# RWKV-7 recurrence with its output by time steps on partitions, group norm along the free axis, and later weight splits

## The chip, the cores and the metric

The kernel runs on one core of one Trainium2 chip. The metric is the device time in microseconds of one execution; the time shown is the median of several runs. The engines have queues of their own, which run in order: TensorE (PE), VectorE (DVE), ScalarE (ACT), GpSimd (POOL), and SyncE (SP), which issues most of the DMAs.

## The reference, cut to what matters

Two decoder layers over 512 prompt tokens and 8 samples of one token each (520 columns, N). Each layer is a norm, one input projection of 53 tiles of 128 output channels, sliding-window attention in 16 heads beside an RWKV-7 recurrence in 16 heads, SiLU gates, and one output projection of 16 tiles. The change touches the recurrence's output and the group norm behind it:

```python
def step(S, inp):
    r_t, w_t, k_t, v_t, kk_t, a_t = inp
    sa = jnp.einsum('bhij,bhj->bhi', S, -kk_t)
    S = (S * w_t[:, :, None, :] + sa[..., None] * (kk_t * a_t)[:, :, None, :]
         + v_t[..., None] * k_t[:, :, None, :])
    return S, jnp.einsum('bhij,bhj->bhi', S, r_t)
...
mu = jnp.mean(ys, axis=-1, keepdims=True)
var = jnp.mean(jnp.square(ys - mu), axis=-1, keepdims=True)
yn = ((ys - mu) * lax.rsqrt(var + GN_EPS)).reshape(Bn, T, RWKV_WIDTH)
yn = yn * ln_w.astype(f32) + ln_b.astype(f32)
bonus = jnp.sum(r_h * k_h * r_k.astype(f32), axis=-1, keepdims=True) * v_h
y_rw = (yn + bonus.reshape(Bn, T, RWKV_WIDTH)).astype(x.dtype)
```

`ys` has 64 channels for each head; the mean and the variance go over them. The result is then multiplied by a gate.

## The kernel before, in words

**The projections.** Activations lie with channels on partitions and the 520 columns along the free axis. Weights come as fp32 blocks of 4 x 128 rows by 128 columns ("quarters", four for each output tile). Each is split into a rounded part `hi` and a rest `lo`; activations are split likewise (`hh`, `hl`; in the output projection `yh`, `yl`). `quarter` (L372 to L387) does 4 x 3 x 2 matmuls of 260 columns in fp32r into an accumulator. After the last one it calls `split_w(n + DEPTH)`: ScalarE casts the `hi` of the quarter after that (L355), VectorE subtracts to give `lo` (L365), SP loads a later one (L347). `lo` has three buffers, `hi` four and the raw blocks four. `held` names quarters of the second layer's first two tiles, which are used in two passes over half the columns, 12 matmuls each.

**The side work.** All else is written as generators (`chain`, `attend`, `attend_samples`, `gate`, `ada` and others) that `Side` threads between the projection's matmuls. After each such matmul but an accumulator's last, `tick` advances a count and runs at most one generator to its next `yield`; the number that it yields is its distance in ticks to its next piece. `W` holds these distances. `drain` runs pieces without matmuls between until a condition holds. So the order of instructions in each engine's queue is written out when the kernel is built, and only data and buffers make engines wait.

**The order of tiles** in a layer: the low-rank tile L, then for each pair of heads p three tiles P (r, k, v), with gate tiles R and A among them, then K, V, K, V, eight Q, and the rest of the gate tiles A. After the tile A3 the kernel goes on through A4 to A7, and drains the last attention and the chains behind A4, and the sample attention behind A7. Then comes the output projection; its first half of input channels are those of the recurrence.

**A chain** (`chain`, from L535) is started for each pair of heads after its third P tile, 16 chains in all; about three are under way at a time. It makes decays and keys, 64 x 64 products (`atp`, L638), the masked `atq` and `atk`, writes `atk` to DRAM and loads it again as `f` on GpSimd's DMA queue (L662), inverts 32 x 32 triangles on GpSimd (L670, L672, in `xi`), sends the inverse back through DRAM into `xT` (L714, L721), and completes it with two groups of small matmuls (`t2a`, L733 and L741) with copies on VectorE between them (L727, L736, L745).

Then it goes through eight blocks of 64 time steps (L747 to L789). In each, `rp` (L763) is the product of the stacked (q, kk) of the block with the state `m0`; only its lower half is read. `sp` (L770) applies the inverse. `mn` (L774) is the update of the state. The output `yp` is made with channels on partitions: L775 has all 128 columns of `sv` as stationary side and `atq` (128 columns) as moving side, and L777 adds the state's part with `m0` stationary. ScalarE copies two 64 x 64 blocks into `y` (L787).

Behind the blocks come the eight samples' states, whose outputs are put into the last 8 columns of `y` (L819, L823). The group norm goes over all 520 columns with channels on partitions: `y` is split, centred by a product with `cmat` (`yc`, four matmuls of 260 columns), squared, split, summed by `bones` (`vp`, four more), and the root is taken on ScalarE as `Ln` and `Exp` (L842, L843). VectorE scales and adds weight, bias and bonus (L845, L847) and multiplies with the gate (L851).

**Buffers.** Most tiles of up to 520 columns come from one ring `t2` of `NW2` buffers; matmul outputs of the side work from four PSUM banks (`ps1`).

Of the kernel before, what the change touches and what calls it, by code (L numbers as in the profile page):

```python
# [27 lines left out]
NW2 = 71  # L28
# [78 lines left out]
DEPTH = 3  # L107
RMS = 29
HQ = 4
LEAD0 = 3  # L110
GA = 1
# [60 lines left out]
def body(ctx, tc, xt, ct, consts, pars, wada, win, wout, lora, sst, swkv, ck, cv, cvn, fing,  # L172
# [62 lines left out]
    bia = cpool.tile([128, 1], F32, name="bia")  # L235
    ve.memset(bia, 64 * GN_EPS)
# [7 lines left out]
    lnw8 = cpool.tile([128, L, 8], F32, name="lnw8")  # L244
    nsk = cpool.tile([128, L, 17], F32, name="nsk")

    def derive(mats):
# [7 lines left out]
        ve.tensor_scalar(out=lnw8, in0=par[:, :, P_LNW:P_LNW + 8], scalar1=8.0, scalar2=None, op0=ALU.mult)  # L255
# [86 lines left out]

    def load_w(n):
# [155 lines left out]
    def layer(l, hh, hl, xprev, xnext, start, prepare, after):  # L499
# [35 lines left out]
        def chain(p, lw, r, kr, v):  # L535
# [55 lines left out]
            ve.scalar_tensor_tensor(out=rk, in0=r, scalar=pc(P_RK), in1=k, op0=ALU.mult, op1=ALU.mult)  # L591
# [36 lines left out]
            atq, atk = [], []  # L628
# [96 lines left out]
            x1 = sm.tile([128, 2, 8, 32], F32, tag="x1", name="x1", bufs=1)  # L725
# [11 lines left out]
            yield W[30]  # L737
# [8 lines left out]
            yield W[31]  # L746
            y = t2([128, N], "y")  # L747
            for c in range(8):
# [11 lines left out]
                yp = ps[:, 384:512].rearrange("p (h t) -> p h t", h=2)  # L760
# [35 lines left out]
            yield W[35]  # L796
# [17 lines left out]
            sy.dma_start(out=o_ss[l, p], in_=st)  # L814
            yield W[38]
            ps = ps1("ys")

            for b in range(0, B, 2):
                pe.matmul(ps[:, 2 * b:2 * b + 4], st[:, b:b + 2].rearrange("p b i -> p (b i)"),  # L819
                          rbd[:, b:b + 2].rearrange("p b h -> p (b h)"), start=True, stop=True)  # L820
            for h in range(2):
                for i in range(2):
                    ve.tensor_copy(y[64 * h:64 * h + 64, T + i:N:2], ps[64 * i:64 * i + 64, 2 * i + h:2 * B:4])  # L823
            yield W[39]

            yh = high(y)
            yield W[40]
            ys = low(y, yh)
            yield W[41]
            ycs = t2([128, N], "ycs")  # L830
            s2 = y
            for h in range(2):
                se.copy(out=ycs[:, h * NH:(h + 1) * NH], in_=sums(cmat, ys, h, "yc"))
                yield W[42]
            se.activation(out=s2, in_=ycs, func=AF.Square)
            s2h = high(s2)
            yield W[43]
            s2s = low(s2, s2h)
            yield W[44]
            vps = [sums(bones, s2s, h, "vp") for h in range(2)]  # L840
            for h in range(2):
# [652 lines left out]
```

## Time and profile before

| | before |
|---|---|
| median of 3 runs | 2344.32 us (2335.37 to 2345.83) |
| profiled execution, its own time | 2349.78 us |
| its span, first to last instruction | 2348.0 us |
| mean granted TensorE clock, of full speed | 0.975 |
| TensorE busy | 2223.8 us, 20708 matmul instructions |
| VectorE busy | 1482.8 us |
| ScalarE busy | 1057.9 us |
| GpSimd busy | 794.7 us |

The rows further down are from that one profiled execution; all their times count from its first instruction. Matmuls are pipelined, so the duration of one is longer than its distance to the next; the distance of starts is what it costs in a stream. An fp32 matmul is two instructions, a transpose and an fp32r matmul one.

### The profile page before, as it was taken

The numbers are of one execution on the slowest core, as the hardware profiler recorded it, in microseconds if no ns is written. First come the engines' busy times: TensorE is split into PE (matmuls) and PEld (weight loads), VectorE is DVE, ScalarE is ACT, GpSimd is POOL, SyncE is SP. The second block draws the span as 40 slices with busy tenths as digits, with TensorE's granted clock in tenths as the row PEclk, the third lists the DMA queues.
The fourth block names the chain that finished last, engine by engine and source line by source line (L and its number), as shares of the span: only waits on it lengthen the run. The fifth ranks groups of instructions, "written<-read, shape, count | busy, mean of one in ns | idle before, by whom it ended". The sixth has DMA issues, their size and how long they took to land. (4 is left out here: it accounts for less than half of the span.)

```text
span 2348.0 us, 53897 instructions
## 1 busy us (share of the span) xinstructions
PE 2223.8 (95%) x20708; PEld 2104.7 (90%) x20708; DVE 1482.8 (63%) x3712; ACT 1057.9 (45%) x2346; POOL 794.7 (34%) x1428
## 2 busy tenths in 40 slices
PE   5999999999999999999999999999999999999997
PEld 4899989999989898889989989889999999899997
DVE  3464677767785886533365456577776778765346
ACT  3244354554455555422244435345555446553222
POOL 2105655766566000000011526655776440000112
PEclk8999999999999999999999999999999999999998
DMA  9945555323333225777762455543332322244335
GB/s 363 348 149 169 166 158 160 104 89 97 102 95 95 64 79 158 225 225 245 244 211 77 129 156 163 165 138 106 94 96 88 96 90 77 60 131 138 113 115 180
DMA packets 229329, 337.92 MB, mean 144 GB/s; under 512 B 59696, under 2 KB 80304, under 8 KB 228912
## 3 DMA queue, kind: packets, MB, share of 16 engines
q1 hardware_dynamic: 223184, 321.89, 44.1%
q0 software_dynamic: 5888, 12.59, 1.8%
q8 instruction: 163, 2.67, 0.5%
q14 instruction: 94, 0.77, 0.1%
HBM read 303.90 MB, written 32.56 MB: 143 GB/s over the span
## 5 line engine op out<-in xcount | busy, mean ns | idle before, releaser
L365 DVE TENSOR_TENSOR lo<-raw,hi 128x512 fp32r<-128x512 f32 x568 | 414.5, 730 | 454.0 <-PE psO L380 135.4
L355 ACT CAST hi<-raw 128x512 fp32r<-128x512 f32 x568 | 350.8, 619 | 632.2 <-PE psP L380 211.2
L380 PE MATMUL psP<-hh,lo 128*128 128x260 f32 x1408 | 307.7, 292 | 0.0
L380 PE MATMUL psP<-hl,hi 128*128 128x260 f32 x1408 | 305.0, 292 | 0.0
L380 PE MATMUL psP<-hh,hi 128*128 128x260 f32 x1408 | 304.1, 292 | 0.2 <-ACT dm L518 0.2
L672 POOL TENSOR_TENSOR xi<-xi,tmp 128x248 f32<-128x248 f32 (+30 forms) x496 | 280.8, 566 | 38.9
L670 POOL TENSOR_TENSOR tmp<-f,xi 128x248 f32<-128x248 f32 (+30 forms) x496 | 258.7, 521 | 86.6 <-DMA f<-d 49.1
L380 PEld LDWEIGHTS psP<-hh,lo 128*128 128x128 f32 x1408 | 225.7, 192 | 6.3 <-issue 3.7
L380 PEld LDWEIGHTS psP<-hl,hi 128*128 128x128 f32 x1408 | 225.1, 192 | 5.9 <-issue 3.3
L380 PE MATMUL psO<-yh,hi 128*128 128x260 f32 x1024 | 225.1, 286 | 3.6 <-DVE xsn L1193 3.6
L380 PEld LDWEIGHTS psP<-hh,hi 128*128 128x128 f32 x1408 | 224.6, 192 | 3.1 <-issue 1.2
L380 PE MATMUL psO<-yh,lo 128*128 128x260 f32 x1024 | 225.2, 286 | 1.7 <-DVE lo L365 1.7
L380 PE MATMUL psO<-yl,hi 128*128 128x260 f32 x1024 | 224.5, 285 | 0.0
L380 PEld LDWEIGHTS psO<-yh,hi 128*128 128x128 f32 x1024 | 166.6, 191 | 5.7 <-issue 5.6
L380 PEld LDWEIGHTS psO<-yh,lo 128*128 128x128 f32 x1024 | 166.7, 191 | 3.6 <-DVE lo L365 1.9
L380 PEld LDWEIGHTS psO<-yl,hi 128*128 128x128 f32 x1024 | 166.6, 191 | 1.6 <-issue 1.6
L1329 POOL TENSOR_SCALAR yo<-xnew,fg 128x260 f32<-128x260 f32 x32 | 31.2, 978 | 391.6 <-DVE xnew L1190 377.4
L445 POOL TENSOR_TENSOR rmsr<-rmsv,mhalf 128x3 f32<-128x3 f32 x6 | 5.6, 938 | 464.4 <-DMA raw<-in_wout_dram 449.3
L787 ACT COPY y<-seq 64x64 f32<-64x64 f32 x256 | 52.6, 205 | 195.5 <-DVE mbd L781 136.1
L299 PE MATMUL adps<-rawa,cT 128*32 128x128 f32 (+1 forms) x2048 | 112.5, 348 | 23.5 <-DMA rawa<-in_wada_dram 23.0
L380 PE MATMUL psQ<-hl,hi 128*128 128x260 f32 x512 | 117.6, 295 | 0.0
L380 PE MATMUL psQ<-hh,lo 128*128 128x260 f32 x512 | 114.3, 294 | 0.0
(362 smaller groups left out, 5463.6 us busy)
## 6 DMA issues: line engine op xcount, KB each, us to landing
raw<-in_win_dram SPq DMA_DIRECT2D x424, 256.0 KB, 3.3
rawa<-in_wada_dram SPq DMA_DIRECT2D x384, 256.0 KB, 4.8
raw<-in_wout_dram SPq DMA_DIRECT2D x152, 256.0 KB, 3.6
f<-d POOLq DMA_DIRECT2D x64, 128.0 KB, 3.6
gd<-th SPq DMA_DIRECT2D x22, 260.0 KB, 2.5
gr<-gd SPq DMA_DIRECT2D x22, 260.0 KB, 3.5
x<-in_xt_dram SPq DMA_DIRECT2D x16, 260.0 KB, 5.3
yd<-rk SPq DMA_DIRECT2D x16, 260.0 KB, 3.4
```

The costliest lines, as they stand in the source:

```text
L299: pe.matmul(ap[32 * g:32 * g + 32, 0:w], cT[:, kk, :], raw[g * w // 512][:, c:c + w], start=(kk == 0), stop=(kk == KT - 1))
L355: se.copy(out=his[n], in_=raws[n])
L365: ve.tensor_tensor(out=lo, in0=raws.pop(n), in1=hi, op=ALU.subtract)
L380: pe.matmul(ps[:, h, 0:NH], a[:, k % 4], b[:, h * NH:(h + 1) * NH], start=(k == k0 and j == 0), stop=stop)
L445: ge.tensor_tensor(out=r[:, 0:3], in0=v[:, 0:3], in1=mhalf[:, 0:3], op=ALU.pow)
L670: ge.tensor_tensor(out=tv, in0=f[:, s:s + 1, s + 1:32].to_broadcast([128, 8, 31 - s]), in1=xi[:, :, s:s + 1].to_broadcast([128, 8, 31 - s] ...
L672: ge.tensor_tensor(out=xi[:, :, s + 1:32], in0=xi[:, :, s + 1:32], in1=tv, op=ALU.add)
L787: se.copy(out=y[hs, 64 * c:64 * c + 64], in_=yp[hs, h])
L1329: ge.tensor_scalar(out=out[h][m // 2][:, m % 2], in0=xn[:, h * NH:h * NH + NH], scalar1=fg[:, m:m + 1], scalar2=None, op0=ALU.mult)
```

## The change

- **Output of a block by time steps.** `ap` has 64 time steps on partitions and 2 x 64 channels along the free axis: for each head a slice of `aqs` of 72 columns (64 of `atq` and 8 beyond) is the stationary side, 64 columns of `sv` the moving one. `aqs` is `atq` with 8 more columns, the last 8 set to zero. L777 goes; the state's part is the upper half of `rp`, which ScalarE copies into `yq`. `y` and `yq` hold block c on partitions 64 (c % 2) and on, at column group c // 2. GpSimd adds them after the eighth block.
- **Group norm along the free axis.** For the 512 prompt columns, mean and variance come from `bn_stats` and `bn_aggr` on VectorE, eight of each, the root from a power on GpSimd, and scale and shift are done by eight `Identity` activations on ScalarE; four transposes bring `y` back to channels on partitions, and one instruction on VectorE scales it and adds it to the bonus `b2`. The 8 samples keep the old way in 8 columns (`ysm`), with the power in place of `Ln` and `Exp`. The factors 0.5, ln_w and ln_b are folded into constants (`hrk`, `hln`, `lnw4`).
- **Weight splits.** `quarter` puts the split on a list `due`; the next quarter carries it out behind its ninth matmul (`LATE`).
- **Distances and buffers.** 40 ticks more ahead of the load of `f`; `W[30]` doubled, `W[31]` times four (the `t2a` groups); `W[35]` + 10, and 8 and 4, around the statistics; the last distances of the chain shorter; `W[79]` tripled for the second `qq` subtraction in `attend`; `W[61]` tripled in `attend_samples`; `GA` 2 in place of 1 (tiles of `ada` loaded ahead for the gate's modulation); `NW2` 72 in place of 71; `x1` moves into the ring.

```diff
-NW2 = 71
+NW2 = 72
...
+LATE = 9
...
-GA = 1
+GA = 2
...
@@ quarter
+        done = 0
         for k in range(4 * key[1], 4 * key[1] + 4):
...
+                    done += 1
+                    if done == LATE and due:
+                        split_w(due.pop())
...
         if key not in held or not halves[0]:
-            split_w(n + DEPTH)
+            due.append(n + DEPTH)
@@ chain
             for g in range(2):
-                atq.append(t2([128, 4, 2, 64], "atq"))
+                aq = t2([128, 520], "atq")
+                ge.memset(aq[:, 512:520], 0.0)
+                aqs.append(aq)
+                atq.append(aq[:, 0:512].rearrange("p (e h t) -> p e h t", e=4, h=2))
...
+            yield 40
             for j in range(4):
                 ge.dma_start(out=f[j:128:4], in_=d1.rearrange("b c s t -> (b c) s t"))
...
-            yield W[30]
+            yield 2 * W[30]
...
-            yield W[31]
-            y = t2([128, N], "y")
+            yield 4 * W[31]
+            y = t2([128, 4, 128], "y")
+            yq = t2([128, 4, 128], "yq")
+            ge.memset(yq[0:64, 0], 0.0)
...
                 if c:
                     pe.matmul(rp, qk[g][:, e].rearrange("p a t -> p (a t)"), m0, start=True, stop=True)
                     ve.tensor_tensor(out=rr[64:128], in0=rp[64:128], in1=sv[g][64:128, e], op=ALU.add)
+                    se.copy(out=yq[ys, c // 2], in_=rp[0:64])
...
-                pe.matmul(yp, sv[g][:, e], atq[g][:, e], start=True, stop=(c == 0))
-                if c:
-                    pe.matmul(yp, m0, qk[g][:, e, 0].unsqueeze(1).to_broadcast([128, 2, 64]), start=False, stop=True)
+                for h in range(2):
+                    o = 128 * e + 64 * h
+                    w = 72
+                    pe.matmul(ap[0:w, 64 * h:64 * h + 64], aqs[g][:, o:o + w], sv[g][:, e, 64 * h:64 * h + 64],
+                              start=True, stop=True)
...
-                for h in range(2):
-                    hs = slice(64 * h, 64 * h + 64)
-                    se.copy(out=y[hs, 64 * c:64 * c + 64], in_=yp[hs, h])
+                se.copy(out=y[ys, c // 2], in_=ap[0:64])
                 yield W[34]
+            ge.tensor_tensor(out=y, in0=y, in1=yq, op=ALU.add)
...
-            yield W[35]
+            yield W[35] + 10
+            for i in range(8):
+                ve.bn_stats(out=st6[:, i], in_=y[:, i // 2, 64 * (i % 2):64 * (i % 2) + 64])
+            yield 8
+            for i in range(8):
+                ve.bn_aggr(out=mv[:, i], in_=st6[:, i])
+            ve.tensor_scalar(out=mv[:, :, 0], in0=mv[:, :, 0], scalar1=-1.0, scalar2=None, op0=ALU.mult)
+            ve.tensor_scalar(out=rs8, in0=mv[:, :, 1], scalar1=GN_EPS, scalar2=None, op0=ALU.add)
+            ge.tensor_tensor(out=rs8, in0=rs8, in1=mhalf, op=ALU.pow)
+            yield 4
+            ge.tensor_tensor(out=mv[:, :, 0], in0=mv[:, :, 0], in1=rs8, op=ALU.mult)
...
+            for i in range(8):
+                yi = y[:, i // 2, 64 * (i % 2):64 * (i % 2) + 64]
+                se.activation(out=yi, in_=yi, func=AF.Identity, scale=rs8[:, i:i + 1], bias=mv[:, i, 0:1])
             yield W[38]
...
+            ps = ps1("yT")
+            for j in range(4):
+                pe.transpose(ps[:, 128 * j:128 * j + 128], y[:, j], ident)
+            ve.scalar_tensor_tensor(out=b2[:, 0:T], in0=ps, scalar=hln[:, l, p:p + 1], in1=b2[:, 0:T], op0=ALU.mult,
+                                    op1=ALU.add)
             yield W[39]
-            yh = high(y)
...
-            ys = low(y, yh)
...
-                se.copy(out=ycs[:, h * NH:(h + 1) * NH], in_=sums(cmat, ys, h, "yc"))
...
-            se.activation(out=s2, in_=ycs, func=AF.Square)
-            s2h = high(s2)
...
-            vps = [sums(bones, s2s, h, "vp") for h in range(2)]
...
-                se.activation(out=s2[:, h * NH:(h + 1) * NH], in_=vps[h], func=AF.Ln, bias=bia[:, 0:1])
-            se.activation(out=s2, in_=s2, func=AF.Exp, scale=-0.5)
...
+            ps = ps1("yc")
+            pe.matmul(ps[:, 0:B], cmat.bitcast(F32), ysm[:, 0], start=True, stop=True)
...
+            pe.matmul(ps[:, 0:B], bones.bitcast(F32), ysm[:, 2], start=True, stop=True)
...
@@ attend
-                yield W[79]
+                yield W[79] * (1 + 2 * u)
@@ attend_samples
-                yield W[61]
+                yield 3 * W[61]
```

## Rows read from the trace of the kernel before

**Rows 1.** The page, part 1: busy time, share of the span, instructions.

```profile
PE 2223.8 (95%) x20708; PEld 2104.7 (90%) x20708; DVE 1482.8 (63%) x3712; ACT 1057.9 (45%) x2346; POOL 794.7 (34%) x1428
```

**Rows 2.** TensorE's waits: for whom, us in total, times, longest.

```profile
PE adps L299 <- DMA rawa<-in_wada_dram: 23.0, 9, 17.7
PE t2a L741 <- DVE x L736: 14.6, 9, 2.2
PE seq L774 <- DVE sv L772: 12.9, 12, 2.0
...
PE sc L949 <- DVE qq L931: 5.6, 7, 2.0
...
PE psS L380 <- DVE part L404: 3.6, 2, 1.8
PE psO L380 <- DVE xsn L1193: 3.6, 2, 1.8
...
PE ssc L1041 <- DMA ktc<-in_ck_dram: 1.8, 1, 1.8
```

**Rows 3.** Two windows: busy by engine, TensorE's granted clock, DMA share, GB/s.

```profile
1625.00:1635.00 10.00, 10.00 (x115) 9.47 (x114) 9.51 (x21) 2.89 (x6) 1.04 (x1) 1.00 0.37 101
1637.60:1641.00 3.40, 3.40 (x31) 3.36 (x24) 1.22 (x4) 0.24 (x1) 1.85 (x4) 0.67 0.62 207
```

**Rows 4.** TensorE's timeline, a block of the recurrence: start, duration, line, shapes, count.

```profile
1616.29 0.38 PE L774 MATMUL seq<-sv,kbt 128*128 128x128 f32 x2
1616.51 0.39 PE L775 MATMUL seq<-atq,sv 128*128 128x128 f32 x2
...
1617.07 0.40 PE L380 MATMUL psP<-hh,hi 128*128 128x260 f32 x2
1617.31 0.40 PE L380 MATMUL psP<-hl,hi 128*128 128x260 f32 x2
```

**Rows 5.** TensorE's timeline, the samples' output (one projection matmul left out).

```profile
329.36 0.95 PE L819 MATMUL ys<-rbd,st 128*128 128x4 f32 x8
...
330.38 0.40 PE L380 MATMUL psP<-hh,hi 128*128 128x260 f32 x2
```

**Rows 6.** TensorE's timeline, the samples' attention (one projection matmul left out).

```profile
2121.09 0.40 PE L1067 MATMUL spo<-sptb,vc 128*64 128x4 f32 x8
...
2121.65 0.40 PE L380 MATMUL psA<-hh,lo 128*128 128x260 f32 x2
```

**Rows 7.** TensorE's timeline, four transposes (two projection matmuls left out).

```profile
889.55 0.60 PE L982 MATMUL pT<-cst,s 128*128 128x128 f32 x4
...
890.23 0.40 PE L380 MATMUL psQ<-hl,hi 128*128 128x260 f32 x2
```

**Rows 8.** ScalarE's timeline, a chain's group norm.

```profile
883.88 1.28 ACT L842 ACT_TABLE_LOAD   x1
...
887.88 0.84 ACT L985 COPY ptb<-pT 128x512 f32<-128x512 f32 x2
```

**Rows 9.** TensorE's timeline at the same place.

```profile
888.50 0.67 PE L993 MATMUL ops<-ptb,vtok 128*64 128x128 f32 x8 [2.12 <-ACT ptb L985]
```

**Rows 10.** VectorE's timeline, second layer's output projection.

```profile
2164.60 0.69 DVE L365 TENSOR_TENSOR lo<-raw,hi 128x512 fp32r<-128x512 f32 x1 [2.20 <-PE psO L380]
2165.21 0.87 DVE L1190 SCALAR_TENSOR_TENSOR xnew<-psO,mod,xo 128x260 f32<-128x260 f32 x2
...
2166.19 0.17 DVE L1194 TENSOR_TENSOR xsn<-xsn,xo 128x8 f32<-128x8 f32 x1
```

**Rows 11.** The chain that ended last, end of the input projection: start, us, what.

```profile
2136.56 0.41 PE pnb L1075 x2
2136.96 4.47 PE psA L380 x37
```

**Rows 12.** GpSimd's timeline between two chains' inversions.

```profile
1556.69 1.04 POOL L659 TENSOR_TENSOR kb<-kb,pend 128x512 f32<-128x512 f32 x1 [4.33 <-issue]
...
1566.45 2.16 POOL L662 DMA_DIRECT2D f<-d  x4 [8.71 <-DMA d<-atk]
```

More of the change, by code (lines that the diff above doesn't have):

```diff
@@ L234, in body @@
     bones, cmat, rotm = sel[:, 0], sel[:, 1], sel[:, 2]
-    bia = cpool.tile([128, 1], F32, name="bia")
-    ve.memset(bia, 64 * GN_EPS)
     mhalf = cpool.tile([128, 8], F32, name="mhalf")
@@ L243, in body @@
     oka = cpool.tile([128, L, 8], F32, name="oka")
-    lnw8 = cpool.tile([128, L, 8], F32, name="lnw8")
+    hrk = cpool.tile([128, L, 8], F32, name="hrk")
+    hln = cpool.tile([128, L, 16], F32, name="hln")
+    lnw4 = cpool.tile([128, L, 8], F32, name="lnw4")
     nsk = cpool.tile([128, L, 17], F32, name="nsk")
@@ L254, in derive @@
         ve.tensor_scalar(out=oka, in0=hka, scalar1=-1.0, scalar2=1.0, op0=ALU.mult, op1=ALU.add)
-        ve.tensor_scalar(out=lnw8, in0=par[:, :, P_LNW:P_LNW + 8], scalar1=8.0, scalar2=None, op0=ALU.mult)
+        ve.tensor_scalar(out=hrk, in0=par[:, :, P_RK:P_RK + 8], scalar1=0.5, scalar2=None, op0=ALU.mult)
+        ve.tensor_scalar(out=hln, in0=par[:, :, P_LNW:P_LNW + 16], scalar1=0.5, scalar2=None, op0=ALU.mult)
+        ve.tensor_scalar(out=lnw4, in0=par[:, :, P_LNW:P_LNW + 8], scalar1=4.0, scalar2=None, op0=ALU.mult)
         ve.tensor_scalar(out=nsk, in0=par[:, :, P_SINK:P_SINK + 17], scalar1=-1.0, scalar2=None, op0=ALU.mult)
@@ L341, in body @@
     raws, his, splits = {}, {}, {}
+    due = []
     def load_w(n):
@@ L590, in chain @@
             rk = t2([128, N], "rk")
-            ve.scalar_tensor_tensor(out=rk, in0=r, scalar=pc(P_RK), in1=k, op0=ALU.mult, op1=ALU.mult)
+            ve.scalar_tensor_tensor(out=rk, in0=r, scalar=hrk[:, l, p:p + 1], in1=k, op0=ALU.mult, op1=ALU.mult)
             yield W[14]
@@ L627, in chain @@
             rks = low(rk, rkh)
-            atq, atk = [], []
+            atq, atk, aqs = [], [], []
             flat = lambda ap: ap.rearrange("p e h t -> p (e h) t")
@@ L723, in chain @@
             yield W[28]
-            x1 = sm.tile([128, 2, 8, 32], F32, tag="x1", name="x1", bufs=1)
+            x1 = t2([128, 2, 8, 32], "x1")
             for i in range(2):
@@ L745, in chain @@
                 ve.tensor_copy(flat(xT[i])[64:96, :, 32:64], pa[o:o + 32, 8:16])
-            yield W[31]
-            y = t2([128, N], "y")
+            yield 4 * W[31]
+            y = t2([128, 4, 128], "y")
+            yq = t2([128, 4, 128], "yq")
+            ge.memset(yq[0:64, 0], 0.0)
+            st6 = sm.tile([128, 8, 6], F32, tag="st6", name="st6", bufs=2)
+            mv = sm.tile([128, 8, 2], F32, tag="mv", name="mv", bufs=2)
+            rs8 = sm.tile([128, 8], F32, tag="rs8", name="rs8", bufs=2)
             for c in range(8):
@@ L759, in chain @@
                 rp, sp, mn = ps[:, 0:128], ps[:, 128:256], ps[:, 256:384]
-                yp = ps[:, 384:512].rearrange("p (h t) -> p h t", h=2)
+                ap = ps[:, 384:512]
+                ys = slice(64 * (c % 2), 64 * (c % 2) + 64)
                 rr = rrs[p % 2]
@@ L820, in chain @@
                           rbd[:, b:b + 2].rearrange("p b h -> p (b h)"), start=True, stop=True)
+            ysm = sm.tile([128, 4, B], F32, tag="ysm", name="ysm", bufs=2)
             for h in range(2):
                 for i in range(2):
-                    ve.tensor_copy(y[64 * h:64 * h + 64, T + i:N:2], ps[64 * i:64 * i + 64, 2 * i + h:2 * B:4])
+                    ve.tensor_copy(ysm[64 * h:64 * h + 64, 0, i:B:2], ps[64 * i:64 * i + 64, 2 * i + h:2 * B:4])
+            ps = ps1("yT")
+            for j in range(4):
+                pe.transpose(ps[:, 128 * j:128 * j + 128], y[:, j], ident)
@@ L824, in chain @@
+            ve.scalar_tensor_tensor(out=b2[:, 0:T], in0=ps, scalar=hln[:, l, p:p + 1], in1=b2[:, 0:T], op0=ALU.mult,
+                                    op1=ALU.add)
             yield W[39]
-            yh = high(y)
+            ps = ps1("yc")
+            pe.matmul(ps[:, 0:B], cmat.bitcast(F32), ysm[:, 0], start=True, stop=True)
+            ve.tensor_copy(ysm[:, 1], ps[:, 0:B])
+            ve.tensor_tensor(out=ysm[:, 2], in0=ysm[:, 1], in1=ysm[:, 1], op=ALU.mult)
             yield W[40]
-            ys = low(y, yh)
@@ L843, in chain @@
-            se.activation(out=s2, in_=s2, func=AF.Exp, scale=-0.5)
-            yield W[45]
-            ve.scalar_tensor_tensor(out=s2, in0=ycs, scalar=lnw8[:, l, p:p + 1], in1=s2, op0=ALU.mult, op1=ALU.mult)
-            yield W[46]
-            ve.scalar_tensor_tensor(out=b2, in0=s2, scalar=pc(P_LNB), in1=b2, op0=ALU.add, op1=ALU.add)
+            ps = ps1("vp")
+            pe.matmul(ps[:, 0:B], bones.bitcast(F32), ysm[:, 2], start=True, stop=True)
+            ve.tensor_scalar(out=ysm[:, 3], in0=ps[:, 0:B], scalar1=64 * GN_EPS, scalar2=None, op0=ALU.add)
@@ L848, in chain @@
+            ge.tensor_tensor(out=ysm[:, 3], in0=ysm[:, 3], in1=mhalf, op=ALU.pow)
+            yield 2 * W[45]
             gr = t2([128, N], "gr")
             sy.dma_start(out=gr, in_=gd[l, :, 8 + p])
-            yield W[47]
-            ve.scalar_tensor_tensor(out=b2, in0=b2, scalar=0.5, in1=gr, op0=ALU.mult, op1=ALU.mult)
+            yield W[45]
+            ve.scalar_tensor_tensor(out=ysm[:, 1], in0=ysm[:, 1], scalar=lnw4[:, l, p:p + 1], in1=ysm[:, 3],
+                                    op0=ALU.mult, op1=ALU.mult)
@@ L852, in chain @@
+            ve.tensor_tensor(out=b2[:, T:N], in0=b2[:, T:N], in1=ysm[:, 1], op=ALU.add)
+            ve.scalar_tensor_tensor(out=b2, in0=b2, scalar=hln[:, l, 8 + p:9 + p], in1=gr, op0=ALU.add, op1=ALU.mult)
             sy.dma_start(out=yd[l, :, p], in_=b2)
```

9 lines of the change are left out of this document (removed).

## The prediction

> **What bounds the kernel now.** I read the page first: TensorE is busy 2223.8 us of a span of 2348.0, VectorE 63%, ScalarE 45%, GpSimd 34% [rows 1]. That leaves TensorE 124.2 us of idle time and makes its queue the bound: time goes away only if its instructions get cheaper, or if it stands still less. Its list of waits [rows 2] says for what it stands: the largest items are single waits of 1 to 2 us behind VectorE, in the side work that is threaded between the projection's matmuls. The windows [rows 3] show a second price of such a stand: in the stretch without one the granted clock is 1.00, in the 3.4 us behind the wait of 1.48 us before the pair of `t2a` matmuls at 1637.08 it is 0.67 in the mean, part of it at the lower of the two levels (1.2 GHz of 2.4). (1.00 - 0.67) x 3.4 = 1.1 us are lost on top. [...]
>
> **1. The recurrence's matmuls.** Durations of matmuls overlap, so I take prices from starts. From 1616.29 to 1617.07 stand three fp32 matmuls of 128 stationary columns by 128 moving ones (L774, L775, L777), two instructions each, and one fp32r matmul of 260 columns, which takes 0.12 (two from 1617.07 to 1617.31) [rows 4]. (0.78 - 0.12) / 3 = 0.22 us each, 0.11 an instruction. A chain (one pair of heads in one layer; 16 in all) now pays L775 eight times and L777 seven times: 15 x 0.22 = 3.30 us. L777 goes, since the product of q with the state is already in the unused upper half of L763's output. In place of L775 come two matmuls of 72 stationary by 64 moving columns in each of 8 steps, 32 instructions. No row has that form. What sets 0.11? In `ys`, 128 stationary columns and only 4 moving ones, eight instructions and one projection matmul take 1.02 us, so (1.02 - 0.12) / 8 = 0.11 too [rows 5]: the stationary side sets it, and fewer moving columns alone would save nothing. In `spo`, 64 stationary columns, eight take (0.56 - 0.12) / 8 = 0.055 [rows 6]. Between these ends I take 0.065, nearest to `spo`, as 72 is near 64: 32 x 0.065 = 2.08 us a chain, -1.22, or **-19.5 us** for 16. With 0.055 it is -24.6; with 0.11, 3.52 a chain, it is +3.5.
>
> The Trainium skill (TensorE: Matmul & The Clock Gate, "LDWEIGHTS (loading the stationary operand)") says that a weight load's time is its columns divided by 1.2 ns, which gives an estimate of 60 ns for 72 columns and -22 us for this part; rows 5 and 6 go the same way.
>
> **2. The group norm on TensorE.** Eight fp32r matmuls of 260 columns leave each chain, 0.96 us. Four transposes come, 0.11 each: (0.68 - 0.24) / 4 [rows 7]; and two fp32 products of 128 stationary by 8 moving columns, four instructions at 0.11 [rows 5]. 0.96 - 0.88 = 0.08 a chain, **-1.3 us**.
>
> **3. The group norm on ScalarE.** Each chain now loads two tables, for `Ln` and `Exp`, 1.28 us each. With the activations they hold ScalarE from 883.88 to 887.88, 4 us, and the attention's `ptb` copy is queued behind them [rows 8]; TensorE waits 2.12 us for it at 888.50 [rows 9]. The same wait stands at 2041.12, and smaller ones of 1.46 and 0.66 elsewhere. The new norm needs no table of its own: eight short `Identity` and 15 copies in place of 16 copies and the eight wide activations and casts. **-7 us**; none of it if the eight `Identity`, waiting for GpSimd's power, block the same queue.
>
> **4. Larger distances.** The second `t2a` group comes 14 ticks (a tick is one projection matmul, 0.12 us) behind VectorE's copy instead of 7: 0.84 us off each of nine waits of 14.6 us together [rows 2], 7.6 us, and with it some of the slow stretches behind them [rows 3]: **-10 us** (0 to -18). The second `qq` subtraction gets 12 ticks more, 1.4 us, against waits of 5.6 us in seven: **-5**. The samples' `ssc` gets 8 ticks against a wait of 1.8 and one of 1.5: **-3**. Two tiles loaded ahead for the gate's modulation: of its 23.0 us, 17.7 are one wait at the start and stay, some 3 us lie in layer 1: **-3**.
>
> **5. Weight splits nine matmuls later.** VectorE and ScalarE are in-order, and now the split of a quarter's weights stands ahead of the read-out of the tile just finished. At 2164.60 `lo` (0.69 us) runs before the residual `xnew`, and TensorE waits for that accumulator [rows 10]; with the late split the read-out goes first. Four such waits, 3.6 + 3.6 us [rows 2], lose 0.7 each, 2.8, and some of their slow stretch: **-5**. The recurrence's own waits (12.9 us in twelve) keep their size in my sum, because VectorE also gets more to do: eight statistics of 64 columns, eight aggregations and nine small instructions, between 0.17 and 0.69 each [rows 10], about 4 us plus one wide add, for four wide ones of some 0.7. That is +2 us a chain, 32 us on an engine idle for 865 us [rows 1]; where the cover is missing, it becomes a recurrence wait. The late `lo` still has 44 matmuls, 5.3 us, before its quarter needs it; the weight DMA behind it on SP's queue starts 1.1 us later and has three quarters of 2.9 us.
>
> **6. What the distances cost.** The sample attention must end before the last gate tile does. Now its last product, `pnb`, has 37 projection matmuls behind it [rows 11]. Eight samples take 8 ticks more each, 64; about 12 are given back where the kernel drains the last attention. So `pnb`, `spo` and the last `spT` fall some 15 ticks past the tile's end, where no matmul covers their hand-overs to ScalarE and VectorE, which have the last gate's `tanh` and products to do: some 2.5 us of waits and one slow stretch [rows 3], 3.5 in each layer, and half a us in the drain: **+8 us**. Nothing past it is late: the first half of the output projection reads other channels.
>
> The longer chain (some 50 ticks more of about 1190) is covered: the last one starts 15 tiles of 95 ticks before its results are drained.
>
> **Sum.** -19.5 - 1.3 - 7 - 10 - 5 - 3 - 3 - 5 + 8 = -45.8. The profiled execution's own time is 2349.8, so 2304.0. That execution is 5.5 above the median of the runs; I take 2 off: **2302 us**.
>
> **The rivals.**
> *The waits come back.* VectorE's extra short instructions put new 1 to 2 us waits where the old ones were, so parts 4 and 5 give nothing: -19.5 - 1.3 - 7 + 8 = -19.8, 2330. For it: nearly all waits in rows 2 are for VectorE, in bursts. Against: the statistics are spread over 22 ticks, and the waits of part 4 get distance of their own.
>
> The Trainium skill (VectorE: DVE Perf Modes, "The TRN2 errata") speaks against the new norm: an instruction from SBUF pays a fixed cost whatever its width, so it advises tiles of 512 elements or more. The trace agrees: 0.17 us for 8 columns, 0.69 for 512 [rows 10]. By that rule eight pieces of 64 columns lose what the transposed form saves, which is this rival.
>
> *72 columns cost what 128 do.* Part 1 is +3.5: 2304 + 23 = 2327. For it: no row has such a form. Against: `spo` [rows 6].
> *Both:* 2330 + 23 = 2353: within 0.5%.
> *GpSimd becomes the pace (slower).* Its queue gets the sum `y + yq` (as `kb`, 1.04 us) and the power between two chains; the power waits for VectorE's aggregation, and the inversion's load `f` is behind it. Now `kb` ends at 1557.7 and `f` is issued at 1566.45 only because its data comes then [rows 12]; with the power, due some 42 ticks after the recurrence's end, I expect it 6 to 8 us later. The consumers are issued 56 ticks later, at least 6.7 us, and the inverse had 7 us to spare (`xT` issued by 1621.65, 3.5 to land, read at 1632.65). So it decides from about 14 us of delay; 20 us would be 6 x 14 chains = 84: 2388.
>
> **Numbers.** Forecast 0.55; waits back 0.24; 72 as 128 0.10; both 0.04; GpSimd 0.07. All bounds at their good ends (-24.6, -1.3, -9, every wait of rows 2 but the start) give about -76, 2270; the two middling rivals reach 2330, with their spread 2333. I take 2272 to 2333, which leaves out GpSimd's case, the double one and the tails. About 0.5% (2332.6) is what a measurement tells from no change: faster takes the forecast, 0.09 of the 72-column case and 0.14 of the waits: 0.78; same 0.15; slower 0.07.
>
> **What would show it.** L775's successor at 0.13 us from start to start in two instructions, not 0.22; 32 more TensorE instructions in all; 32 fewer table loads; `t2a` and `sc` nearly gone from TensorE's waits; new waits on `spo` and `pnb` at the end of both input projections; GpSimd's `f` later by 6 to 8 us without a wait at `t2a`. Wrong would make me: `seq` waits above 25 us, waits on `lo`, or `Identity` on ScalarE waiting long for GpSimd.

## The result, and the profile after

The changed kernel takes 2355.30 us, the median of seven runs (2350.56 to 2359.50), the kernel before beside it 2340.43; the ratio is 1.0064, 95% interval 1.0049 to 1.0080. Slower, by about 15 us, where 2302 was forecast. The profiled execution has a span of 2354.6 us and a mean granted clock of 0.978; the one before, 2348.0 us long at 0.975, was some 9 us slower than that kernel's median of seven. Part 1 of its page, to be read against [rows 1]:

```profile
PE 2203.9 (94%) x20740; PEld 2085.8 (89%) x20740; DVE 1501.7 (64%) x4033; ACT 992.6 (42%) x2298; POOL 874.8 (37%) x1540
```

TensorE is busy 19.9 us less, in 32 more instructions, near the 20.8 that the first two parts of the sum said (measured by starts, part 1 alone gives less, see below). But its idle time is 2354.6 - 2203.9 = 150.7 us, against 124.2: +26.5. The difference of the two, +6.6, is the whole difference of the spans. So the question is what it now waits for. TensorE's list of waits (us in total, times, longest), against [rows 2]:

```profile
PE seq L792 <- ACT yq L786: 40.6, 24, 3.4
PE adps L302 <- DVE acc L439: 17.4, 1, 17.4
PE seq L796 <- DVE sv L794: 14.9, 15, 2.5
PE adT L314 <- ACT asb L309: 7.9, 6, 6.0
PE seq L792 <- issue: 5.8, 5, 1.3
...
PE psS L386 <- DVE wlo L370: 3.9, 2, 3.3
PE psO L386 <- DVE lo L370: 3.7, 4, 1.6
PE t2a L755 <- DVE x L750: 3.4, 6, 0.8
...
PE pnb L1109 <- DVE z L1105: 3.2, 2, 2.0
```

The second `t2a` group fell from 14.6 to 3.4 us, and the waits of `sc`, `ops` and `xsn` have left the head of the list. The 17.4 us at L302 are the wait at the program's start, for which [rows 2] have 17.7 under a DMA's name. At the head stands a wait that the kernel before didn't have: the recurrence's product `sp` (L792) for ScalarE's copy of q's product (L786), 40.6 us. The reader should stop at this line, since `sp` doesn't use what that copy writes: its operand is `rr`, which VectorE makes. The timelines of ScalarE, VectorE and TensorE at one of these places (start, duration, line, in brackets idle before and for whom):

```profile
305.29 0.60 ACT L360 CAST hi<-raw 128x512 fp32r<-128x512 f32 x1
305.91 1.28 ACT L596 ACT_TABLE_LOAD   x1
307.21 0.64 ACT L596 ACTIVATE rn<-rn 128x520 f32<-128x520 f32 x1
307.86 1.28 ACT L597 ACT_TABLE_LOAD   x1
309.15 0.64 ACT L597 ACTIVATE rn<-rn 128x520 f32<-128x520 f32 x1
309.70 0.24 ACT L786 COPY yq<-seq 64x128 f32<-64x128 f32 x1
```

```profile
306.67 0.69 DVE L1146 SCALAR_TENSOR_TENSOR th<-th,psR 128x520 f32<-128x520 f32 x1
307.40 0.29 DVE L785 TENSOR_TENSOR rr<-seq,sv 64x128 f32<-64x128 f32 x1
```

```profile
309.99 0.79 PE L792 MATMUL seq<-rr,xT 128*128 128x128 f32 x2 [3.37 <-ACT yq L786]
310.44 0.57 PE L386 MATMUL psP<-hl,hi 128*128 128x260 f32 x1
310.80 0.64 PE L386 MATMUL psP<-hh,lo 128*128 128x260 f32 x2
```

`rr` is done at 307.69, but `sp` starts at 309.99, when ScalarE has worked through the next chain's `Ln` and `Exp` with a table load of 1.28 us each, and made the copy. `rp`, which the copy reads, and `sp` lie in one PSUM tile, `seq`, and so in one bank (no run here tells the tile from the bank), and here the program keeps the engines' accesses to a bank in order. Eleven of the 24 waits stand behind such a pair of table loads, 2.2 to 3.4 us each, 33.1 us in all, and in them `rr` had been done for 1.4 to 2.3 us. So not all of the 40.6 us is the bank's: counted wait by wait from the end of `rr`, some 23 us are, and in the other 17 `rr` itself wasn't there yet. The price doesn't end with the wait: afterwards the main matmuls start 0.22 us apart for some 2.5 us (310.80 and on, two of them 0.43), the lower level of the clock (the granted clock is 0.50 from 310.40 to 312.80), where [rows 4] have 0.12.

The kernel before had such an order too, in a place where it cost nothing. Its ScalarE list of waits had this line, though VectorE's `mbd` reads another part of the bank than ScalarE's copy of y:

```profile
ACT y L787 <- DVE mbd L781: 136.1, 65, 4.9
```

There ScalarE waited, and TensorE's list has no wait for that copy. In the changed kernel TensorE waits.

The Trainium skill (PSUM — Partial Sum Buffer, "PSUM bank collisions raise a hardware error") asks for this order: engines have to be kept apart by bank and group of 32 partitions, not by address. The waits at L792, 40.6 us, are that order as this program keeps it; what happens without it no run here shows.

### The profile page after: what moved, and what is told of

It is laid out like the page before. It is cut to its first block, busy times and chain, and to the rows that moved or that the text cites. A ratio compares the mean times of both kernels' runs of the same rounds, so it can differ in the third digit from the quotient of the medians.

```text
span 2354.6 us, 54013 instructions
## 1 busy us (share of the span) xinstructions
PE 2203.9 (94%) x20740; PEld 2085.8 (89%) x20740; DVE 1501.7 (64%) x4033; ACT 992.6 (42%) x2298; POOL 874.8 (37%) x1540
## 4 chain that ended last, share of the span: by engine, by line
PE 69%; DVE 12%; POOL 6%; DMA 5%; ACT 4%; issue 3%; SPq 0%; DVEq 0%; POOLq 0%; ACTq 0%
PE psP L386 15%; PE psO L386 15%; PE psA L386 7%; PE psR L386 6%; PE psQ L386 4%; PE psS L386 4%; PE adps L302 3%; POOL xi L686 2%; POOL tmp L684 2%; DVE lo L370 2%; PE atp L651 1%; DMA rawa<-in_wada_dram 1%; PE seq L792 1%; PE psK L386 1%; PE seq L796 1%
## 5 line engine op out<-in xcount | busy, mean ns | idle before, releaser
L370 DVE TENSOR_TENSOR lo<-raw,hi 128x512 fp32r<-128x512 f32 x568 | 409.7, 722 | 223.1 <-PE psO L386 103.5
L686 POOL TENSOR_TENSOR xi<-xi,tmp 128x248 f32<-128x248 f32 (+30 forms) x496 | 273.7, 552 | 38.9
L684 POOL TENSOR_TENSOR tmp<-f,xi 128x248 f32<-128x248 f32 (+30 forms) x496 | 250.2, 504 | 79.6 <-DMA f<-d 44.2
L809 ACT COPY y<-seq 64x128 f32<-64x128 f32 x128 | 33.0, 258 | 287.8 <-DVE mbd L805 230.7
L302 PE MATMUL adps<-rawa,cT 128*32 128x128 f32 (+1 forms) x2048 | 106.4, 342 | 21.3 <-DVE acc L439 17.4
L386 PE MATMUL psQ<-hh,hi 128*128 128x260 f32 x512 | 115.4, 292 | 0.0
```

The lines of the kernel that those rows point to most:

```text
L302: pe.matmul(ap[32 * g:32 * g + 32, 0:w], cT[:, kk, :], raw[g * w // 512][:, c:c + w], start=(kk == 0), stop=(kk == KT - 1))
L370: ve.tensor_tensor(out=lo, in0=raws.pop(n), in1=hi, op=ALU.subtract)
L386: pe.matmul(ps[:, h, 0:NH], a[:, k % 4], b[:, h * NH:(h + 1) * NH], start=(k == k0 and j == 0), stop=stop)
L684: ge.tensor_tensor(out=tv, in0=f[:, s:s + 1, s + 1:32].to_broadcast([128, 8, 31 - s]), in1=xi[:, :, s:s + 1].to_broadcast([128, 8, 31 - s] ...
L686: ge.tensor_tensor(out=xi[:, :, s + 1:32], in0=xi[:, :, s + 1:32], in1=tv, op=ALU.add)
L809: se.copy(out=y[ys, c // 2], in_=ap[0:64])
```

## The experiments

Each is timed against the kernel before on the same chip, so ratios are compared (in brackets the 95% interval); 0.001 is 2.3 us. "The second kernel" is that of run 2, and so on; a run's parent is the kernel that its edit starts from. In the expectations theory A is the bank, B, where one is named, the later weight split, C that VectorE has more to do, and D, formed after the first four, that the chain's length decides what VectorE is doing when a block needs it.

**1. The copy at the block's end, on ScalarE.**

```diff
-                    se.copy(out=yq[ys, c // 2], in_=rp[0:64])
...
+                if c:
+                    se.copy(out=yq[ys, c // 2], in_=rp[0:64])
```

> The changed kernel with ScalarE's copy of the state's part (yq) moved from behind the first product of a block to the block's end, beside the copy of y; nothing else. Theory A (the copy reads the PSUM bank into which TensorE writes the next product, so the recurrence's matmul L792 waits for ScalarE's whole queue, 49.6 us in all, and some 14 us of slow clock follow): waits at L792 under 6 us, time 2285 to 2305 us, ratio to the kernel before 0.976 to 0.985. Theory B (the splits nine matmuls late make the loss: lo and wlo late, SP's DMAs late): no change, 2345 to 2360. Theory C (VectorE's and GpSimd's short instructions of the new group norm make it): waits move to L796 and L784, 2335 to 2355.

2340.3 us, 0.9993 (0.9975 to 1.0012). The wait for the copy is gone, but 17.8 us at `sp` behind VectorE's `rr` and 19.7 at `mn` behind `sv` stand in its place. The bank was a cause, and a smaller one than I now expected.

**2. The copy on VectorE.**

```diff
-                    se.copy(out=yq[ys, c // 2], in_=rp[0:64])
+                    ve.tensor_copy(yq[ys, c // 2], rp[0:64])
```

> The changed kernel with the copy of yq in its place, but done by VectorE behind its own sum rr. Theory A in its form that the length of ScalarE's queue is the cost: L792 waits only for VectorE, 0.3 us later than the sum, hidden by 13 ticks; 2295 to 2315 us. In its form that any second reader of the bank costs: L792 still waits over 25 us, 2330 to 2355. Theory B and C: 2345 to 2370 (VectorE has 112 copies of 0.25 us more).

2335.4 us, 0.9978 (0.9965 to 0.9992). Its waits at `sp` are 33 us, 24.3 of them for this copy.

**3 and 4. The late split alone: taken back in the changed kernel, and put into the kernel before.**

```diff
-            due.append(n + DEPTH)
+            split_w(n + DEPTH)
```

> The changed kernel with the weight splits handed out at the quarter's end again, as before the change; the copy of yq stays. Theory A: L792 keeps its 50 us of waits; 2345 to 2365, 0 to 10 us worse or better than the changed kernel. Theory B: the loss goes, 2295 to 2325, waits on lo and wlo (7.6 us) go.

> The kernel before with the late splits alone (LATE = 9). Theory A, by my own term of -5 us for them: 2328 to 2342, ratio 0.995 to 1.0. Theory B: over 2350, ratio over 1.004, and waits on lo and wlo of some 8 us appear.

Without it the changed kernel takes 2350.6, 1.0045 (1.0023 to 1.0067); with it the old one 2340.3, 0.9994 (0.9976 to 1.0012). Neither differs from its parent by more than the intervals. Part 5's 5 us aren't there, though run 4's interval alone would still hold them (see run 14).

**5 and 6. The chain's distances: taken back in the second kernel, and put into the kernel before (20 ticks ahead of `f` in place of 40; the other two as in the change).**

```diff
-            yield 40
...
-            yield 2 * W[30]
+            yield W[30]
...
-            yield 4 * W[31]
+            yield W[31]
```

> The changed kernel with the copy of q's product on VectorE, and the chain's own larger distances taken back (no 40 ticks ahead of f, W[30] and W[31] once each), so that a chain is 56 ticks shorter. Parent: 2335 us, 42 us of waits in the recurrence behind VectorE (24 at sp, 18 at mn), 4 us at t2a. Theory D (phase): the 56 ticks put each recurrence beside the next chain's wide VectorE work; without them the recurrence's waits fall to 25 us or less, t2a's come back to 12 to 15, and the time is 2325 to 2333. Theory C (VectorE has simply more to do in a chain): the recurrence's waits stay at 35 or more, t2a's come back, and the time rises to 2342 to 2348.

> The kernel before with only the chain's distances made larger: 20 ticks (not 40) ahead of f, W[30] twice, W[31] four times, 36 ticks in all. The prediction's part 4: t2a's waits go from 14.6 to about 4 us and 8 to 10 us of the time go with them, 2331 us, the recurrence's waits staying at 14 us. Theory C says the same, as VectorE's work is the old one. Theory D: the recurrence's waits behind VectorE grow from 14 to 25 or more, and the time stays within 5 us of 2341 or is longer.

The first takes 2358.1, 1.0077 (1.0054 to 1.0100), 23 us more than its parent; the second 2334.8, 0.9978 (0.9962 to 0.9993), 5 less. Theory D as I had put it falls, and so does C as put: in run 5 the recurrence's waits fell to 21.0 us where it said 35 or more, and the time rose beyond its range. But the lists are telling. The first kernel's:

```profile
PE seq L795 <- DVE sv L793: 18.9, 14, 2.1
PE t2a L754 <- DVE x L749: 17.7, 11, 2.7
...
PE t2a L746 <- DVE x L740: 13.1, 12, 2.0
```

and the second's:

```profile
PE seq L775 <- DVE sv L773: 10.5, 16, 1.8
PE seq L764 <- DVE mbd L782: 9.2, 12, 1.6
...
PE t2a L734 <- DVE x L728: 7.2, 9, 1.7
```

With the new recurrence and the old distances, `sp` waits 0.2 us where it had waited 33, and `t2a` 30.8 where it had waited 4: the wait has moved, and got dearer. It got dearer by the clock, not by idle time: TensorE stands still 140.9 us against 139.4, but is busy for 2215.8 against 2190.3, at a clock of 0.966 in the mean against 0.987.

**7 and 8. VectorE's load: seven of eight statistics left out (all slices are normalised with the first one's), and y's sum made by VectorE in each block in place of ScalarE's copy and GpSimd's sum.** Both from the second kernel.

```diff
-            for i in range(8):
+            for i in range(1):
                 ve.bn_stats(out=st6[:, i], in_=y[:, i // 2, 64 * (i % 2):64 * (i % 2) + 64])
...
+            ve.tensor_copy(mv[:, 1:8], mv[:, 0:1].to_broadcast([128, 7, 2]))
```

```diff
-                se.copy(out=y[ys, c // 2], in_=ap[0:64])
+                if c:
+                    ve.tensor_tensor(out=y[ys, c // 2], in0=ap[0:64], in1=yq[0:64, c % 4], op=ALU.add)
+                else:
+                    ve.tensor_copy(y[ys, c // 2], ap[0:64])
...
-            ge.tensor_tensor(out=y, in0=y, in1=yq, op=ALU.add)
```

> The parent of the first run (copy of q's product on VectorE), with seven of each chain's eight bn_stats and seven of its eight bn_aggr left out and replaced by one copy of the first result (so the norm is computed with the first slice's statistics throughout). It takes about 25 us off VectorE. Theory C: the recurrence's waits fall from 42 to 30 or less and the time to 2320 to 2326. Theory D: these instructions stand after the recurrence, so its waits change by less than 5 us and the time stays at 2332 to 2338.

> The parent of the first run, with y and q's product added by VectorE in each block as it reads y from PSUM, so that ScalarE's copy of y and GpSimd's wide sum go. VectorE gets 128 instructions of about 0.28 us and loses the slowdown of sa (1.34 to 0.70 us, 10 us); GpSimd loses 23 us; ScalarE 33 us. Theory C: with 26 us more on VectorE inside the recurrence the waits at sp and mn grow by 5 to 10 us, 2340 to 2348. Theory D: VectorE's amount of work doesn't matter by itself; the bank's wait of ScalarE's copy behind mbd goes and GpSimd is freed, 2328 to 2336.

2323.1, 0.9930 (0.9910 to 0.9950), with VectorE busy 1513.2 us instead of 1531.4; and 2348.5, 1.0034 (1.0016 to 1.0052), with 1546.6. So 18 us less on VectorE went with 11 us less time, and 15 more with 13 more. Both signs are theory C's, but run 7 doesn't show its mechanism, that the recurrence's waits behind VectorE fall to 30 us. The two of the second kernel

```profile
PE seq L792 <- DVE yq L786: 24.3, 21, 2.0
PE seq L796 <- DVE sv L794: 18.1, 23, 2.5
```

are nearly as long in the seventh:

```profile
PE seq L792 <- DVE yq L786: 23.8, 22, 2.0
PE seq L796 <- DVE sv L794: 17.5, 22, 2.4
```

What went are 6.0 us at `sp` for which the list names nothing ("issue": 0.2 are left) and the 4.2 at `t2a`. In run 8 the two grow from 42.4 to 47.3 us, as theory C has it.

**9. A bank of its own for `rp`.** ScalarE keeps the copy; only the meeting in the bank is taken away.

```diff
-                rp, sp, mn = ps[:, 0:128], ps[:, 128:256], ps[:, 256:384]
+                sp, mn = ps[:, 128:256], ps[:, 256:384]
...
                 if c:
+                    rp = ps1("rp")[:, 0:128]
```

> The changed kernel with one difference: the product rp gets a PSUM tile, and so a bank, of its own, so that ScalarE's copy of q's half of it and the product sp no longer meet in one bank. ScalarE still makes the copy. Theory A (the bank orders sp behind ScalarE's copy): TensorE's 40.6 us of waits at sp for that copy are gone; what is left at sp is VectorE's rr, 15 to 25 us, and the time is that of the copy on VectorE, 2332 to 2342. Rival (ScalarE's late copy delays the recurrence in some other way, as through the tile's release or its own queue): the waits stay at 35 or more and the time at 2348 or more.

2333.2 us, 0.9972 (0.9956 to 0.9988). The same place in the chain, ScalarE and TensorE:

```profile
308.75 1.28 ACT L597 ACT_TABLE_LOAD   x1
310.05 0.64 ACT L597 ACTIVATE rn<-rn 128x520 f32<-128x520 f32 x1
310.59 0.24 ACT L787 COPY yq<-rp 64x128 f32<-64x128 f32 x1
```

```profile
305.57 0.38 PE L785 MATMUL rp<-mbd,qk 128*128 128x128 f32 x2
308.58 0.49 PE L793 MATMUL seq<-rr,xT 128*128 128x128 f32 x2 [1.06 <-DVE rr L786]
```

The copy is as late as before, 2.0 us after `sp` has started, and `sp` waits 1.06 us for its true operand instead of 3.37. The shared bank is shown as the cause of the wait for the copy, and priced: (1.0064 - 0.9972) x 2341 = 21.5 us, some 5 either way. The list of waits has left

```profile
PE seq L793 <- DVE rr L786: 18.4, 17, 1.7
PE seq L797 <- DVE sv L795: 16.3, 19, 2.4
```

which the kernel before had at 0 and 12.9.

**10 to 12. 20 ticks ahead of `f` in the second kernel; `sp` 4 ticks later in its block, with the last stretch 4 shorter; and 20 ticks with a bank of its own.**

```diff
-            yield 40
+            yield 20
```

```diff
-                    yield W[32] + 4
+                    yield W[32] + 8
...
-                yield W[34]
+                yield W[34] - 4 * (c < 7)
```

> The changed kernel with the copy of q's product on VectorE and 20 ticks ahead of f in place of 40. With 40: 2335 us, sp waits 33 us, t2a 4. With none, and W[30], W[31] once: 2358 us, sp 0, t2a 31. Theory D2 (the chain's length sets what VectorE is doing when a recurrence block needs it, so the waits at sp go with the length, while t2a's go with its own two distances, which stay): sp 3 to 15, t2a under 8, 2318 to 2330. Rival (the chain's length is not what matters; the waits at sp come with VectorE's load): sp stays near 30 and the time near 2335.

> The kernel of the run before with sp's product 4 ticks (0.48 us) later behind rp, and each block's last stretch 4 ticks shorter, so that the chain keeps its length. If sp's waits are short lateness of VectorE's rr, they shrink by 0.4 us each and nothing else moves: 3 to 10 us off the parent. If the waits only move on, those of rp for VectorE's mbd grow by as much (from 2 to 8 us or more) and the time stays within 5 us of the parent.

> Own bank for rp, the copy on ScalarE, and 20 ticks ahead of f: both cures together, with VectorE 32 us less busy than in the second run. Theories A and D2: as the second run or up to 8 us below it, 2312 to 2328, the shortest of all. If the waits at sp come with VectorE's load alone it is 2330 to 2340.

2334.2, 0.9970 (0.9954 to 0.9986); 2338.6, 0.9997 (0.9980 to 1.0015); 2328.0, 0.9943 (0.9924 to 0.9962). The last is the shortest kernel that computes the reference, 13 us under the kernel before. In the first, `sp` is nearly free and two others have its waits:

```profile
PE seq L796 <- DVE sv L794: 21.6, 18, 2.6
...
PE seq L784 <- DVE mbd L805: 15.1, 10, 2.8
...
PE seq L792 <- DVE yq L786: 3.0, 8, 0.5
```

Room for `sp` within the block comes back as waits of `rp` for `mbd` (15.1 to 19.5 us) and helps nothing. All waits of the recurrence and of `t2a` together, from their own lists: before 39.5 us (19.8 + 19.7), sixth kernel 30.2 (23.0 + 7.2), changed 70.5 (66.5 + 4.0), second 57.7, fifth 51.8, ninth 52.3, tenth 46.8, twelfth 47.0. With the bank's wait away, the new chain keeps 47 to 58 us at every length tried, where the old one had 30 to 40, and the length deals them out. Their sum doesn't give the time: run 5 has 6 us less of them than run 2, and takes 23 us more.

**13 to 16. Single terms, each with its own bank for `rp` (parent: the ninth): 128 stationary columns for the first of a block's two products of y; the split at once; the distances outside the chain as before (`W[79]`, `W[61]`, `GA`); GpSimd's sum left out, so that y lacks q's product with the state.**

```diff
-                    w = 72
+                    w = 72 if h else 128
```

```diff
-            due.append(n + DEPTH)
+            split_w(n + DEPTH)
```

```diff
-GA = 2
+GA = 1
...
-                yield W[79] * (1 + 2 * u)
+                yield W[79]
...
-                yield 3 * W[61]
+                yield W[61]
```

```diff
-            ge.tensor_tensor(out=y, in0=y, in1=yq, op=ALU.add)
```

> Own bank for rp (parent: 2333 us), with the first of each block's two products of y fed 128 stationary columns in place of 72 (128 such products, 256 instructions). The prediction's part 1: the stationary side sets the price, 0.065 us at 72 and 0.11 at 128 columns, so the output's matmuls get 256 x 0.045 = 11.5 us dearer, 2345. Rival (72 cost what 128 do, or the 64 moving columns set the price): no change, 2330 to 2336.

> Own bank for rp, and the weight split handed out at once again, as in the kernel before. The prediction's part 5: the late split is worth 5 us, so this takes 2338. Rival, after the two runs that changed it alone (0.9994 in the old kernel, some 5 us gained by undoing it in the changed one): it is worth nothing or costs, 2326 to 2333.

> Own bank for rp, and the distances outside the chain as before: W[79] and W[61] once each, GA 1. The prediction's parts 4 and 6 for these: 5 + 3 + 3 gained and 8 lost, 3 us in all, so this takes 2336, with the waits on sc and ops back (10 us) and those on pnb and spo gone (4 us). Rival (waits return elsewhere): within 3 us of 2333 though the list of waits changes so.

> Own bank for rp, with GpSimd's wide sum of y and q's product left out (so y lacks the product of q and the state). GpSimd loses 23 us, and VectorE's sa, which runs beside the sum, should go from 1.32 to 0.70 us, 10 us off VectorE. Theory C (VectorE's load makes the waits): 4 to 8 us less, 2325 to 2329, and the one wait behind the sum at adT (4.7 to 6 us) goes as well. Rival (the sum is hidden): 2331 to 2336.

- 13: 2333.4, 0.9976 (0.9958 to 0.9994): within the intervals of its parent, where 11.5 us were expected. The starts tell more. TensorE's timeline at a block's end, first the thirteenth kernel, then the changed one:

```profile
1640.18 0.46 PE L801 MATMUL seq<-sv,atq 128*128 128x64 f32 x4
1640.45 0.48 PE L386 MATMUL psP<-hl,hi 128*128 128x260 f32 x2
```

```profile
1660.12 0.41 PE L800 MATMUL seq<-sv,atq 128*72 128x64 f32 x4
1660.34 0.49 PE L386 MATMUL psP<-hl,hi 128*128 128x260 f32 x2
```

  0.27 against 0.22 us for the four instructions. From each start to the next, in medians over all 128 blocks, they take 58, 112, 65 and 37 ns in the thirteenth kernel and 56, 65, 65 and 38 in the changed one. So the stationary side counts, by 49 ns a block, 6.3 us in all and not 11.5; the median time can't tell 6 us from nothing here.
- 14: 2338.6, 0.9981 (0.9961 to 1.0001): +2 us against the parent, inside the intervals. Weighted by their intervals, runs 3, 4 and 14 together put the late split's gain at 0.2 us, 3 either way.
- 15: 2349.5, 1.0032 (1.0016 to 1.0048): 14 us longer, where I had netted them at 3. `sc` is back with 8.2 us, `pnb`'s 3.2 are gone.
- 16: 2335.4, 0.9979 (0.9960 to 0.9998), with VectorE 11.6 us less busy. `sa`, which had run beside the sum, goes from a median of 1705 to 685 ns, and the time doesn't move. Here theory C fails.

```profile
L818 DVE TENSOR_TENSOR sa<-st,smp x16: 681/685/997, 320.7 to 2002.2; 128x512 f32<-128x512 f32 x16
```

**17 and 18. The statistics as two sums along the free axis, of y and of ScalarE's square of it; from the twelfth kernel, and from the ninth.**

```diff
-                ve.bn_stats(out=st6[:, i], in_=y[:, i // 2, 64 * (i % 2):64 * (i % 2) + 64])
...
+            se.activation(out=yq, in_=y, func=AF.Square)
+            ve.tensor_reduce(out=mv[:, :, 0], in_=y8(y), axis=AX.X, op=ALU.add)
...
-                ve.bn_aggr(out=mv[:, i], in_=st6[:, i])
+            ve.tensor_reduce(out=mv[:, :, 1], in_=y8(yq), axis=AX.X, op=ALU.add)
...
```

> The shortest so far (own bank, 20 ticks ahead of f: 2328, 0.9943) with the statistics as two sums along the free axis, of y and of its square by ScalarE, in place of eight bn_stats and eight bn_aggr: some 1 us less on VectorE in each chain, 16 us in all, and 0.6 us more on ScalarE. Theory C (the statistics' short instructions cost waits, 11 us when seven of eight were left out): two thirds of it, 2318 to 2324. Rival (it was the copy, not the load, or ScalarE's square holds its queue behind GpSimd's sum): 2326 or more.

> The same statistics with the change's own 40 ticks ahead of f (parent: own bank alone, 2333, 0.9972). Theory C: 2322 to 2329. Rival: 2331 or more.

2341.3, 1.0003 (0.9992 to 1.0015), 14 us more than its parent; and 2335.7, 0.9970 (0.9949 to 0.9990), the same as its parent. VectorE was not relieved (1491.7 us against 1492.8, and 1508.3 against 1505.7), so they don't test theory C as I had meant. The 14 us at equal load (3.9 of it idle time, 8.9 busy time in the profiled pair, with the clock at 0.978 instead of 0.983) go with 16 more instructions on ScalarE and another order of the rest; from the ninth kernel the same edit costs nothing, so the 14 us come from where instructions fall, and which of them is open.

## Why the prediction was wrong, step by step

**The step that failed** is part 3, and with it the sentence in part 5 that the recurrence's own waits "keep their size". Part 3 read [rows 8] rightly, a ScalarE held for 4 us by two table loads and what waits behind them, and counted as gain that one such group goes: table loads fell from 65 to 33, and the waits of `ops` went. It didn't ask who is now queued behind the other group, the next chain's `Ln` and `Exp` at L596 and L597, which stays. The change put ScalarE's copy there, and the shared bank put TensorE behind the copy: 40.6 us of waits, some 23 of them the bank's own, 21.5 us of time (run 9). I looked for the data that each instruction uses and not for the tile that it lies in; the line of ScalarE's waits quoted above had it.

**The rest of the miss.** The forecast was 53 us too low, so the bank is less than half of it. Part 1 lacks 4.9 us and part 5 its 5. Some 20 more are in the recurrence and `t2a`: with its own bank the kernel waits 52.3 us there, where the sum had left 31.9 (39.5 less part 4's 7.6). That is the size of the second failed step, and its cause is open, as said below.

**Part 1** was right in kind, but the gain is 14.6 us, not 19.5. Taken as the prediction took it, from the group's first start to the second projection matmul behind it, less 0.12, the three old matmuls take 670 ns in the median block, 0.22 each as put, and the new form 528. Less the 0.22 of the state's update that stands first in it, that is 305 ns for the four new instructions: 0.076 each, where 0.065 was put. A chain gains 7 x 142 ns in its blocks with both old products and loses 81 ns in its first block: 0.91 us, times 16.

**Part 4** was too small. Run 6 gives 5 us for 36 of the chain's 56 ticks in the old kernel; with the new recurrence all of them are worth 23 (run 5 against 2), nearly all of it as busy time at a lower clock, and the others, with part 6's cost in it, 14 instead of 3 (run 15). `pnb` did fall past the tile's end and waits 3.2 us in two, as part 6 said.

**Part 5**: nothing measurable, three times (runs 3, 4, 14). The two waits for `xsn` at an accumulator, 3.6 us, did go with the late split, and are back in runs 3 and 14; waits for `lo` and `wlo` took their place, 7.6 us in the changed kernel against 3.1 in run 3.

**What was left at nothing**, VectorE's added work, wasn't covered. Without ScalarE's copy in the way the recurrence and `t2a` wait 47 to 58 us, where the sum had left some 32. That was the rival in which the waits come back; its price, 2330 (2328 with the 2 us that the forecast took off), is near what runs 2, 9 and 10 give (2333 to 2335), but it isn't what happened, which had the bank on top. The nearness is in part luck: in that rival the larger distances give nothing, and runs 5 and 15 show 23 and 14 us for them. How much of these waits VectorE's load makes stays open: in runs 7 and 8 the time goes with the load, but in run 7 the waits behind VectorE hardly change; run 16 takes load away and gains nothing, and run 17 moves 14 us at the same load.

**GpSimd** was as forecast: `f` is issued behind the power and its product, 17.0 us after a chain's last `atp` in the median, against 9.5, without a wait of note at `t2a`. It became the pace once, in the second layer, where VectorE's statistics wait for the sum and TensorE then waits 6.0 us at `adT`; run 16 takes that wait away and gains nothing.

Of my own signs, 32 more instructions, 32 fewer table loads, and `t2a` and `sc` nearly gone were right; of the new waits at the projections' ends `pnb`'s came and `spo`'s didn't (1.1 us, 1.6 before). All three that were named as what would make me wrong came: `seq` waits above 25 us, at 66.5; waits on `lo`, with `wlo` 7.6 us against 1.7; and `Identity` on ScalarE waiting for GpSimd, though of TensorE's waits near those places just one, of 1.6 us, is for ScalarE:

```profile
ACT y L851 <- POOL mv L829: 12.3, 4, 5.4
```

## What to carry to other kernels

For each new read of a PSUM tile, list who else touches the same bank until the tile is freed, and what stands ahead of the reader in its own queue: its lateness is then theirs. Give such a product a bank of its own before giving it distance. A larger distance in one place of a long threaded chain moves the later parts against everything else; before calling a wait gone, look at all the chain's hand-overs, and at the granted clock too, since the same idle time can cost more (run 5).

## What the runs showed of the hardware that was not expected

- With 64 moving columns too the stationary columns count in an fp32 instruction's price on TensorE: within a group the distance of starts is 65 ns for 72 and 112 for 128. The whole group is dearer than that: four instructions of 72 columns cost 305 ns in the changed kernel, and two of them made 128 wide add 49.
- A group of fp32 matmuls hides part of its cost behind its end: in the median block its last instruction is 31 to 38 ns ahead of the first projection matmul, and that one 204 ahead of the second, where 120 is usual.
- GpSimd's power of 128x8 elements takes 1.84 us in the mean, where one of 128x3 took 0.94 in the kernel before and 1.16 in the changed one; its add of 128x512 takes 1.43, and VectorE's multiply of 128x512 beside that add 1.71 us in the median instead of 0.69.
- Two kernels with nearly the same load on VectorE and GpSimd and the same matmuls lie 14 us apart (runs 12 and 17), less of it in TensorE's idle time (3.9 us in the profiled pair) than in its busy time (8.9).
